# Split-weight buffers 32 bytes longer: their starting places run through the multiples of 32 within 128

## The chip, the cores and the metric

The kernel runs on one core of a Trainium2 chip. The metric is the device time of one execution in microseconds (us), the median of three runs. One further execution was taken with the hardware profiler; all rows below are from that one.

## What is computed

The reference is a two-layer decoder trunk in float32 on 256 tokens of width 2048. Each layer normalises its input, multiplies it by `w_in`, runs eight heads of latent attention and eight heads of retention, joins them through `w_o`, and adds a squared-ReLU MLP of width 8192:

```python
for l in range(DEPTH):
    h = rmsnorm(x, attn_norm[l])
    proj = h @ w_in[l]
    c_q, c_kv, k_rope, rq, rk, rv, rg = jnp.split(proj, split_pts, axis=-1)
    a = mla_attention(c_q, c_kv, k_rope, q_norm[l], kv_norm[l], w_uq[l], w_ukv[l], cos64, sin64)
    r = retention(rq, rk, rv, rg, cos128, sin128)
    mixed = jnp.concatenate([rmsnorm(a, beta_attn[l]), r * beta_ret[l]], axis=-1)
    x = x + mixed @ w_o[l]
    h = rmsnorm(x, mlp_norm[l])
    x = x + jnp.square(jax.nn.relu(h @ w_up[l])) @ w_down[l]
return rmsnorm(x, final_norm)
```

## The kernel before

Activations lie transposed in SBUF, features on the partitions, 256 tokens along the row. To keep float32 accuracy with a fast matmul format (float32r), every operand is split into a head and a remainder. A weight block of 512 KB is loaded into one of five `raw` buffers, ScalarE writes its head (L195) and VectorE its remainder (L196) into one of six rotating buffers `w`, each 2048 elements long plus 2 * MOVING = 32 elements of room; one more buffer, `wh`, has 1024 plus 32. TensorE then runs three kinds of matmul on them, and it does this in the order in which the code is written, with the weights of the next matmul loaded (PEld) while the present one runs:

- L229 and L230 (`mac_feat`), always as a pair: the weights in `w` are the stationary operand of 128 columns, and the activations move: 512 columns (head and remainder of the activations, head of the weights), then 256 columns (remainder of the weights). The moving tiles are `xs` (normalised input, also under the name `ms` in the code), `u` (MLP activations), `mix`, `cq` and `ckv`.
- L234 and L235 (`mac_tok`), also a pair of 512 and 256 columns, but the other way round: `w` moves, and `xs` or `ckv` is stationary. L383 to L385 do likewise with 320 columns.
- L730 (`seven_products`): `w` or `wh` moves in runs of 512 columns, and `u` or the sums `f` of it are stationary. 21 such matmuls make a step. Only here the weights lie MOVING = 16 elements (64 bytes) behind the start of their buffer.

L850 is a run of matmuls near the end that read `u` as both operands and whose result nobody uses.

Tiles are placed one behind the other, in the order of their pools, at multiples of 32 bytes. The places that matter are therefore given as the start within 128 bytes (the address modulo 128, as the built program has it). Before the change:

| tile | place before | place after |
|---|---|---|
| `x`, `xs`, `tab`, `ssq` | 96 | 96 |
| `raw` | 64 | 64 |
| `w`, the six buffers | 64, 64, 64, 64, 64, 64 | 64, 96, 0, 32, 64, 96 |
| `wh` | 64 | 0 |
| `w` and `wh` as L730 reads them | 64 bytes further than the two rows above | 64 bytes further |
| `sq`, `t`, `tb` (temporaries) | 64 | 32 |
| `u`, `f`, `mix`, `cq`, `ckv`, `p` and other tiles of a layer | 96 | 64 |

Within a `w` buffer every slice that a matmul reads starts at a multiple of 512 bytes, so all of them have the place of their buffer.

Of the kernel before, what the change touches and what calls it, by code (L numbers as in the profile page):

```python
# [12 lines left out]
F32R = mybir.dt.float32r  # L13
# [5 lines left out]
P = 128  # L19
# [27 lines left out]
MOVING = 16  # L47
# [46 lines left out]
def kernel(ctx: ExitStack, tc: tile.TileContext, xt, positions, w_in, w_uq, w_ukv, w_o, w_up, w_down,  # L94
# [5 lines left out]
    wpool = ctx.enter_context(tc.tile_pool(name="w", bufs=1))  # L100
# [10 lines left out]
    def tmp(tag="t", bufs=6):  # L111
        return tpool.tile([P, T], F32, tag=tag, name=tag, bufs=bufs)


    def w_tile(shape, moving=False):
        n = math.prod(shape[1:])
        o = MOVING if moving else 0
        tag, size, bufs = ("wh", 1024, 1) if moving and n <= 1024 else ("w", max(n, 2048), N_SPLIT)
        t = wpool.tile([P, size + 2 * MOVING], F32R, tag=tag, name=tag, bufs=bufs)[:, o:o + n]
        names = "abc"[:len(shape) - 1]  # L120
        return t.rearrange(f"p ({' '.join(names)}) -> p {' '.join(names)}", **dict(zip(names, shape[1:])))

# [93 lines left out]
    def stream(w, r0, c0, nk, width=256, kc=None, backward=False):  # L216

        kc = kc or 1024 // width
        for s in reversed(range(0, nk, kc)) if backward else range(0, nk, kc):
            raw = early.pop(0) if early else w_load(w[r0 + s * P:r0 + (s + kc) * P, c0:c0 + width], [P, kc, width])  # L220
            ws = w_tile([P, kc, 2, width])
            split_w(ws[:, :, 0, :], ws[:, :, 1, :], raw)
            for k in range(kc):
                yield s + k, ws[:, k]
            weave()
# [125 lines left out]
    for l in range(DEPTH):  # L351
        g0 = l * G_LAYER

        with tc.tile_pool(name=f"mix{l}", bufs=1) as ap:
# [13 lines left out]
            for c0 in range(COL_CQ, COL_CKV, 256):  # L368
                for ps in proj_feat(w_in[l], 0, c0, xs, backward=l > 0):
                    t = tmp()  # L370
# [74 lines left out]

            def mla(i):
                wr = w_tile([P, 4, 2, P])
                wn = []
                for kk in range(0, 4, 2):
                    raw = w_load(w_uq[l][kk * P:(kk + 2) * P, i * 384:(i + 1) * 384], [P, 2, 384])  # L450
                    wu = raw.rearrange("p k (h c) -> p k h c", h=2)
                    ws = w_tile([P, 2, 2, 256])
                    wv = ws.rearrange("p k s (h c) -> p k s h c", h=2)
                    for k in range(2):
                        wrv = wr[:, kk + k].rearrange("p s (a h c) -> p s a h c", a=2, h=2)
                        src = wu[:, k, :, 128:192].rearrange("p h (a c) -> p a h c", a=2)
                        split_w(wrv[:, 0], wrv[:, 1], src)
                    split_w(wv[:, :, 0], wv[:, :, 1], wu[:, :, :, 0:128])
                    wn += [ws[:, 0], ws[:, 1]]
# [187 lines left out]
            for c0, nt in OUT_GROUPS:  # L647
                for n, ps in enumerate(proj_feat(w_o[l], 0, c0 * P, mixed, nt)):
                    j = c0 + n
                    t = tmp()  # L650
# [241 lines left out]
```

## Time and profile before

| | |
|---|---|
| median of three runs | 2172.16 us (2171.9 to 2172.17) |
| profiled execution | 2172.12 us |
| its span, first to last instruction | 2170.3 us |
| TensorE busy | 2135.7 us, 98% |
| VectorE busy | 1789.4 us, 82% |
| ScalarE busy | 1300.3 us, 60% |
| mean granted TensorE clock | 0.994 of full speed |

About 2 us lie outside the span. A matmul's listed duration includes the time in which its results drain, during which the next matmul already runs. How fast TensorE goes is therefore read from the distance between the starts of matmuls, and the listed durations say only how forms compare.

### The profile page before, as it was taken

The numbers are of one execution on the slowest core, as the hardware profiler recorded it, in microseconds if no ns is written. First come the engines' busy times: TensorE is split into PE (matmuls) and PEld (weight loads), VectorE is DVE, ScalarE is ACT, GpSimd is POOL, SyncE is SP. The second block draws the span as 40 slices with busy tenths as digits, with TensorE's granted clock in tenths as the row PEclk, the third lists the DMA queues.
The fourth block names the chain that finished last, engine by engine and source line by source line (L and its number), as shares of the span: only waits on it lengthen the run. The fifth ranks groups of instructions, "written<-read, shape, count | busy, mean of one in ns | idle before, by whom it ended". The sixth has DMA issues, their size and how long they took to land.

```text
span 2170.3 us, 32892 instructions
## 1 busy us (share of the span) xinstructions
PE 2135.7 (98%) x11926; PEld 1861.6 (86%) x11926; DVE 1789.4 (82%) x3183; ACT 1300.3 (60%) x2234; POOL 107.0 (5%) x130
## 2 busy tenths in 40 slices
PE   7999999999999999999899999999999999999997
PEld 6888888888888888888688888888888888888886
DVE  8878976788689779879968888676986887898797
ACT  7455545565676566566645555456665655665665
POOL 4000000001001001100000000000010010010000
PEclk9999999999999999999999999999999999999998
DMA  7555456658757857855465555566587577577663
GB/s 247 171 161 174 147 189 196 184 168 227 235 165 216 241 165 217 247 176 173 148 200 159 165 173 165 183 189 186 169 236 219 167 224 236 165 217 224 181 194 107
DMA packets 364771, 412.69 MB, mean 190 GB/s; under 512 B 14144, under 2 KB 284608, under 8 KB 364608
## 3 DMA queue, kind: packets, MB, share of 16 engines
q1 hardware_dynamic: 349824, 397.08, 59.7%
q0 software_dynamic: 13824, 12.59, 3.9%
q8 instruction: 93, 1.52, 0.3%
q10 hardware_dynamic: 960, 0.92, 0.1%
q14 instruction: 70, 0.57, 0.1%
HBM read 395.85 MB, written 2.10 MB: 183 GB/s over the span
## 4 chain that ended last, share of the span: by engine, by line
PE 88%; DVE 7%; ACT 2%; issue 1%; DMA 1%; SPq 0%; DVEq 0%; ACTq 0%
PE mm L229 43%; PE mm L230 22%; PE mm L730 11%; PE mm L234 3%; DVE w L196 2%; DVE raw L716 2%; PE mm L235 1%; PE at L229 1%; ACT w L195 1%; DMA raw<-w_down 1%; PE at L230 1%; PE at L500 0%; PE at L499 0%; PE mm L383 0%; PE mm L384 0%
## 5 line engine op out<-in xcount | busy, mean ns | idle before, releaser
L195 ACT CAST w<-raw 128x1024 fp32r<-128x1024 f32 (+2 forms) x856 | 847.1, 1007 | 656.8 <-PE mm L230 363.2
L196 DVE TENSOR_TENSOR w<-raw,w 128x1024 fp32r<-128x1024 f32 (+2 forms) x856 | 987.1, 1170 | 291.9 <-ACT w L195 286.1
L229 PE MATMUL mm<-xs,w 128*128 128x512 f32 x2944 | 1034.2, 394 | 8.5 <-ACT w L195 8.3
L230 PE MATMUL mm<-xs,w 128*128 128x256 f32 x2944 | 827.4, 281 | 4.4 <-DVE w L196 4.4
L229 PEld LDWEIGHTS mm<-xs,w 128*128 128x128 f32 x2944 | 553.8, 188 | 127.8 <-ACT w L195 8.6
L230 PEld LDWEIGHTS mm<-xs,w 128*128 128x128 f32 x2944 | 556.0, 189 | 7.5 <-DVE w L196 7.1
L229 PE MATMUL mm<-u,w 128*128 128x512 f32 x1024 | 360.7, 393 | 0.2 <-ACT w L195 0.2
L230 PE MATMUL mm<-u,w 128*128 128x256 f32 x1024 | 288.8, 282 | 6.4 <-DVE w L196 6.4
L229 PEld LDWEIGHTS mm<-u,w 128*128 128x128 f32 x1024 | 193.2, 189 | 43.0 <-ACT w L195 0.7
L230 PEld LDWEIGHTS mm<-u,w 128*128 128x128 f32 x1024 | 194.0, 189 | 10.0 <-DVE w L196 7.3
L730 PE MATMUL mm<-w,f 128*128 128x512 f32 x768 | 191.1, 396 | 2.2 <-ACT w L195 1.2
L716 DVE TENSOR_TENSOR raw<-raw 128x512 f32<-128x512 f32 x256 | 176.8, 691 | 6.6
L229 PE MATMUL mm<-mix,w 128*128 128x512 f32 x512 | 178.0, 391 | 0.0
L730 PEld LDWEIGHTS mm<-w,f 128*128 128x128 f32 x768 | 144.0, 188 | 38.9 <-ACT w L195 2.1
L820 POOL DMA_DIRECT2D x<-t x96 | 83.4, 869 | 1863.0 <-ACT t L819 1561.9
L230 PE MATMUL mm<-mix,w 128*128 128x256 f32 x512 | 143.7, 281 | 0.0
L247 ACT COPY tb<-mm 128x256 f32<-128x256 f32 x232 | 82.5, 371 | 63.0 <-PE mm L230 59.3
L229 PEld LDWEIGHTS mm<-mix,w 128*128 128x128 f32 x512 | 96.1, 188 | 20.8
L730 PE MATMUL mm<-w,u 128*128 128x512 f32 x384 | 110.6, 396 | 0.0
L248 DVE TENSOR_TENSOR t<-mm,tb 128x256 f32<-128x256 f32 x232 | 91.4, 418 | 19.9 <-ACT tb L247 19.4
L230 PEld LDWEIGHTS mm<-mix,w 128*128 128x128 f32 x512 | 96.4, 188 | 0.0
L234 PE MATMUL mm<-w,xs 128*128 128x512 f32 x256 | 92.8, 401 | 0.0
(202 smaller groups left out, 1955.3 us busy)
## 6 DMA issues: line engine op xcount, KB each, us to landing
raw<-w_up SPq DMA_DIRECT2D x256, 512.0 KB, 4.4
raw<-w_down SPq DMA_DIRECT2D x256, 512.0 KB, 5.2
raw<-w_in SPq DMA_DIRECT2D x144, 512.0 KB, 4.5
raw<-w_o SPq DMA_DIRECT2D x64, 512.0 KB, 4.1
x<-t POOLq DMA_DIRECT2D x96, 128.0 KB, 5.7
raw<-w_uq SPq DMA_DIRECT2D x16, 384.0 KB, 4.3
raw<-w_in SPq DMA_DIRECT2D x16, 320.0 KB, 3.2
raw<-w_ukv SPq DMA_DIRECT2D x8, 512.0 KB, 4.3
```

The costliest lines, as they stand in the source:

```text
L195: nc.scalar.copy(dst_h, src)
L196: nc.vector.tensor_tensor(dst_l, src, dst_h.bitcast(F32), op=ALU.subtract)
L229: nc.tensor.matmul(ps, wk[:, 0, n0:n0 + P], act.rearrange("p s t -> p (s t)"), start=first, stop=False)
L230: nc.tensor.matmul(ps[:, 0:T], wk[:, 1, n0:n0 + P], act[:, 0, :], start=False, stop=last)
L234: nc.tensor.matmul(ps, act[:, 0, t0:t0 + P], wk, start=first, stop=False)
L235: nc.tensor.matmul(ps[:, 0:256], act[:, 1, t0:t0 + P], wk[:, 0], start=False, stop=last)
L247: nc.scalar.copy(tb, ps[:, T:2 * T])
L248: nc.vector.tensor_tensor(dst, ps[:, 0:T], tb, op=ALU.add)
L716: nc.vector.tensor_tensor(dst, dst, other, op=ALU.add)
L730: nc.tensor.matmul(ps[i], a[:, p, :], w[:, q, :], start=first and n == 0, stop=last and n == 2)
L820: nc.gpsimd.dma_start(x[j], t, accum_op=ALU.add)
```

## The change

`w_tile` makes each buffer 8 elements (32 bytes) longer. A `w` buffer was 2080 elements or 8320 bytes, which is 65 times 128, so all six had one place within 128. It is 8352 bytes now, and each buffer starts 32 bytes further within 128 than the one ahead of it. Everything that is placed behind the buffers moves by 7 * 32 = 224 bytes, that is 96 within 128; what stands ahead of them stays. The table above has the places that come of it. Nothing else is changed: on every engine the same instructions stand in the same order, with the same sizes, waits and transfers.

```diff
@@ -116,7 +116,7 @@
         n = math.prod(shape[1:])
         o = MOVING if moving else 0
         tag, size, bufs = ("wh", 1024, 1) if moving and n <= 1024 else ("w", max(n, 2048), N_SPLIT)
-        t = wpool.tile([P, size + 2 * MOVING], F32R, tag=tag, name=tag, bufs=bufs)[:, o:o + n]
+        t = wpool.tile([P, size + 2 * MOVING + 8], F32R, tag=tag, name=tag, bufs=bufs)[:, o:o + n]
         names = "abc"[:len(shape) - 1]
         return t.rearrange(f"p ({' '.join(names)}) -> p {' '.join(names)}", **dict(zip(names, shape[1:])))
```

## Rows read from the trace of the kernel before

**Rows 1.** The page's head: span, busy time of each engine, granted TensorE clock.

```profile
span 2170.3 us, 32892 instructions
...
PE 2135.7 (98%) x11926; PEld 1861.6 (86%) x11926; DVE 1789.4 (82%) x3183; ACT 1300.3 (60%) x2234; POOL 107.0 (5%) x130
...
PEclk9999999999999999999999999999999999999998
```

**Rows 2.** The page's chain that ended last, shares of the span.

```profile
PE 88%; DVE 7%; ACT 2%; issue 1%; DMA 1%; SPq 0%; DVEq 0%; ACTq 0%
```

**Rows 3.** The waits of TensorE, longest first: us in total, times, longest.

```profile
PE mm L230 <- DVE w L196: 10.8, 6, 6.4
PE mm L229 <- ACT w L195: 8.5, 3, 7.3
```

**Rows 4.** Groups by form, TensorE: count | busy us, mean ns | idle before.

```profile
L229 PE MATMUL mm<-xs,w 128*128 128x512 f32 x2944 | 1034.2, 394 | 8.5 <-ACT w L195 8.3
...
L229 PE MATMUL mm<-u,w 128*128 128x512 f32 x1024 | 360.7, 393 | 0.2 <-ACT w L195 0.2
...
L730 PE MATMUL mm<-w,f 128*128 128x512 f32 x768 | 191.1, 396 | 2.2 <-ACT w L195 1.2 <-DVE w L196 1.0
L229 PE MATMUL mm<-mix,w 128*128 128x512 f32 x512 | 178.0, 391 | 0.0
...
L730 PE MATMUL mm<-w,u 128*128 128x512 f32 x384 | 110.6, 396 | 0.0
L234 PE MATMUL mm<-w,xs 128*128 128x512 f32 x256 | 92.8, 401 | 0.0
...
L730 PE MATMUL mm<-wh,u 128*128 128x512 f32 x192 | 55.2, 396 | 0.0
L229 PE MATMUL at<-cq,w 128*128 128x512 f32 x96 | 34.6, 393 | 0.0
...
L234 PE MATMUL at<-w,ckv 128*128 128x512 f32 x32 | 11.6, 394 | 0.0
L229 PE MATMUL at<-ckv,w 128*128 128x512 f32 x32 | 11.5, 393 | 0.0
```

**Rows 5.** Timeline, TensorE, sixteen pairs of L229, L230: start us, us.

```profile
700.99 0.39 PE L229 MATMUL mm<-u,w 128*128 128x512 f32 x1
701.22 0.28 PE L230 MATMUL mm<-u,w 128*128 128x256 f32 x1
...
706.55 0.86 PE L730 MATMUL mm<-wh,u 128*128 128x512 f32 x3
```

**Rows 6.** Timeline, TensorE, two runs of eight pairs of L234, L235.

```profile
212.73 0.39 PE L234 MATMUL mm<-w,xs 128*128 128x512 f32 x1
...
215.53 0.39 PE L234 MATMUL at<-w,ckv 128*128 128x512 f32 x1
...
216.93 0.39 PE L234 MATMUL mm<-w,xs 128*128 128x512 f32 x1
...
219.75 0.39 PE L499 MATMUL at<-kn,qn 128*128 128x128 f32 x2
```

**Rows 7.** Chain in order of time, steps of L730: start us, us, count.

```profile
858.26 4.92 PE mm L730 x21
...
879.21 4.88 PE mm L730 x21
```

**Rows 8.** Timeline, TensorE, the run of L850 near the end.

```profile
2149.30 3.15 PE L850 MATMUL mm<-u,u 128*128 128x512 f32 x13
2152.29 0.28 PE L230 MATMUL mm<-u,w 128*128 128x256 f32 x1
```

**Rows 9.** Groups by form, VectorE.

```profile
L189 DVE TENSOR_TENSOR u<-t,u 128x256 fp32r<-128x256 f32 x128 | 50.4, 420 | 0.0
L196 DVE TENSOR_TENSOR wh<-raw,wh 128x512 fp32r<-128x512 f32 x64 | 43.8, 685 | 0.0
...
L196 DVE TENSOR_TENSOR w<-raw,w 128x512 fp32r<-128x512 f32 x16 | 11.0, 685 | 0.8 <-ACT w L195 0.8
```

## The prediction, made before the result was known

> **What bounds the kernel now.** I read the head of the page first: TensorE is busy 98% of the span, VectorE 82%, ScalarE 60%, and the granted clock is at its upper level, 2.4 GHz, in nearly every slice [rows 1]. Then the chain that ended last: 88% of it is TensorE [rows 2]. Then what TensorE waits for: the two longest entries, both for a split of weights, are 19.3 us together in nine stops [rows 3], under 1% of the span. So the time is the sum of the distances between the starts of matmuls, and nothing else can shrink or grow much without passing through them.
>
> How large is such a distance, against the columns alone? A pair of L229 and L230 streams 512 + 256 = 768 columns, 320 ns at 2.4 GHz. Sixteen pairs start from 700.99 to 706.55 us [rows 5], 5.56 / 16 = 347.5 ns a pair. So 27.5 ns of a pair are not columns. A step of L730 has 21 matmuls in 4.88 to 4.92 us [rows 7], 232.4 to 234.3 ns each, 233.3 in the middle, against 213.3 ns for 512 columns: 20.0 ns over. L850 ran 13 matmuls of 512 columns from 2149.30 to 2152.29 us [rows 8], 230.0 ns each.
>
> So matmuls of one size do not have one distance, and what differs between the lines is which tile moves, which one is stationary, and the places of both. I sort them by one number, the place of the moving tile less the place of the stationary one, modulo 128 (the table of places gives it): 96 - 64 = 32 for all pairs of L229 and L230; 0 - 96, which is also 32, for L730; 0 for L850; 64 - 96, that is 96, for L234 and L235. Two runs of eight pairs of L234 take 2.80 and 2.82 us [rows 6], 350.0 and 352.5 ns, although their columns are those of L229's pairs. That is 2.5 and 5.0 ns more, 3.75 in the middle. L850 against L730 is 3.3 ns less. Neither comparison is clean: in L234 the tiles also have exchanged their roles, and L850 runs where little else does. But the sizes bound what a place can be worth here: some ns of a pair of 347.
>
> **The change, part by part.** No instruction, transfer or wait is added, removed or moved, so there are only places to price.
>
> *VectorE, ScalarE, transfers.* The split of 512 elements takes 685 ns with its output at place 64 (`w`) and 685 ns at place 0 (`wh`), and 420 ns for 256 elements with tiles at 64 and 96 [rows 9]. I see no dependence on the place and cost this at nothing. Place 32 for the temporaries is in no row here; should it cost some per cent of these operations, the cover is VectorE's idle 18% and ScalarE's 40% of the span [rows 1]. `raw` and `x`, into which weights and inputs are loaded, keep their places.
>
> *The pairs of L229 and L230.* With `xs` moving there are 2944 of them; with `u`, `mix`, `cq` and `ckv` 1024 + 512 + 96 + 32 = 1664 [rows 4]. The six buffers are taken in turn, so a sixth of the pairs falls to each. With `xs` at 96 the distances of places become 32, 0, 96, 64, 32, 0: a third of the pairs (981) stays at 32, 1472 come to 0 or 64, 491 come to 96. With `u` and the others at 64 they become 0, 96, 64, 32, 0, 96: 832 at 0 or 64, 555 at 96, 277 still at 32.
>
> A pair that comes to 96 costs 3.75 ns more by the rows of L234: (491 + 555) * 3.75 ns = 3.9 us. For pairs at 0 or 64 no row exists. Below: the 512-column part alone was 3.3 ns cheaper at 0 than at 32 in the other pattern (L850 against L730), so a gain of 3.3 ns is not excluded. Above: 5.0 ns, the worse run of L234. Between these I take a loss of 2.5 ns, nearer to the upper end, because L234 alternates 512 and 256 columns as these pairs do, and L850 does not; its row is the farther one. That is (1472 + 832) * 2.5 ns = 5.8 us, with ends of -7.6 and +11.5 us.
>
> *L730.* `u` and `f` go to 64. Of its 768 + 384 = 1152 matmuls on `w` [rows 4], the moving slice is at 0, 32, 64, 96, 0, 32, so the distance becomes 64, 96, 0, 32, 64, 96. The 192 on `wh` come to 0. At 0 I take L850's distance, 3.3 ns less: (192 + 192) * 3.3 = -1.3 us. At 64 and 96 (768 matmuls) the bounds are -3.3 and +5.0 ns, that is -2.5 and +3.8 us, from the same rows; I take nothing, since they have both signs and neither row is nearer.
>
> *L234 and L235.* 256 + 32 = 288 pairs [rows 4] leave the distance 96 in two thirds of the cases. 43 with `xs` and 11 with `ckv` come to 32 and regain 3.75 ns each, the rest some 1 ns: -0.4 us.
>
> **The sum:** 3.9 + 5.8 - 1.3 - 0.4 = +8.0 us. The profiled execution took 2172.12 us, so 2180.1 us; it stands 0.04 us under the median of the three runs, so I forecast 2180 us for the median, 0.4% slower. A slower TensorE gives the splits more time, so some of the 19.3 us of waits may shrink; I count none of it, since they are nine long stops and not many short ones.
>
> **The rivals.**
>
> *The places do not matter (2172 us).* The 2.5 to 5.0 ns of L234 could belong to the exchange of roles and not to the places, and L850's to its quiet surroundings. Then every pair stays at 347.5 ns, every matmul of L730 at 233.3, and the time is 2172. For it speaks that no line here shows two places of the same tile side by side. Against it: the rows differ by up to 5 ns at equal columns and at the same clock, and an exchange of roles would need a reason of its own. The same result comes if losses and gains cancel, or if the unknown distances cost nothing: then 3.9 - 1.3 - 0.4 = +2.2 us, 2174. The Trainium skill, page "TensorE: Matmul & The Clock Gate", section "Step-by-step: what each phase is for", has a rule that speaks for this rival: TensorE has two independent read ports, so "Loading the next tile's weights doesn't steal SBUF read bandwidth from the running matmul". By that rule a stationary tile's place could not change the distance and the sum would be zero; this trace does not decide it, but 27.5 ns over the columns in each pair sit badly with it.
>
> *The unknown distances are the better ones (2166 us, faster).* If 0 and 64 gain in the pairs what L850 shows against L730, the 2304 pairs gain 7.6 us and the 768 matmuls of L730 at 0 or 64 gain 2.5 us; the pairs at 96 still lose 3.9 us. The sum is -6.2 us, 2166 us. It decides from the point where a pair at 0 or 64 gains 2.5 ns: 2304 * 2.5 ns = 5.8 us, with L730's 2.5 us, less 3.9 us, are 4.4 us, 0.2%. For it speaks the one row at distance 0; against it, that it is another pattern of columns.
>
> *Pairs at 0 or 64 are much worse (2199 us).* The mean listed duration of L234 is 401 ns against 391 for L229 with `mix` [rows 4], 10 ns; a part of that is waiting. If 0 or 64 cost 10 ns a pair, 2304 pairs lose 23 us, and with the 3.9 us of the others the time is 2199. For it speaks that the moving and the stationary stream would then meet at the same place from the first column on; against it, again L850, which does so at 230.0 ns.
>
> **How the numbers follow.** Forecast of a small loss, 2176.5 to 2187: 0.46. No effect, or effects that cancel: 0.28. Faster: 0.16. Much slower: 0.10. Two executions of one kernel differ by far less than 0.2% (4.3 us), but a difference under that is about what a measurement of this kernel cannot tell from no change. So faster has 0.16, same 0.28, slower 0.46 + 0.10 = 0.56. The range from 2165 to 2194 us reaches over the faster case, and on the other side to the worst of the forecast (11.5 us for 0 and 64, 5.2 for 96 at 5.0 ns, 3.8 in L730, about 20 us) and a little more; it leaves out the much slower case, and the tail of the faster one.
>
> **What would show it.** In the profile after, runs of L229 and L230 should have two or three distances, by the buffer that holds the weights: 347.5 ns for buffers whose place is 32 under the moving tile's, and around 350 to 352 for the others, changing with each block of weights. L234's runs should come down to 347.5 ns for one buffer in six. L730's steps should spread wider than 4.88 to 4.92 us. VectorE's and ScalarE's mean durations should stay within 1%. The forecast is wrong if all pairs keep one distance, if they fall under 347.5 ns, or if VectorE's or ScalarE's operations grow and TensorE's waits with them.

## The result

The changed kernel takes 2183.47 us, median of four runs (2183.31 to 2183.87), against 2172.16 us: the ratio is 1.0051, with a 95% interval of 1.0038 to 1.0063. That is slower by about 11.3 us, on the side that was forecast and inside the range; the forecast was 8 us.

The page of the kernel after, its head: span, busy time of each engine, and the chain that ended last.

```profile
span 2181.6 us, 32892 instructions
...
PE 2146.9 (98%) x11926; PEld 1862.7 (85%) x11926; DVE 1790.4 (82%) x3183; ACT 1302.7 (60%) x2234; POOL 108.0 (5%) x130
...
PEclk9999999999999999999999999999999999999998
...
PE 90%; DVE 6%; ACT 2%; issue 1%; DMA 1%; SPq 0%; DVEq 0%; ACTq 0%
```

The span has grown by 2181.6 - 2170.3 = 11.3 us [rows 1], and TensorE's busy time by 11.2 us. VectorE's grew by 1.0 us and ScalarE's by 2.4 us. TensorE's growth alone is that of the span, so the difference lies there, at the same granted clock (0.994 before, 0.995 after). Its waits for splits have hardly changed, 12.4 + 7.4 = 19.8 us now against 19.3 before [rows 3]:

```profile
PE mm L230 <- DVE w L196: 12.4, 5, 6.4
PE mm L229 <- ACT w L195: 7.4, 2, 7.1
```

The groups by form of VectorE and ScalarE after:

```profile
L196 DVE TENSOR_TENSOR w<-raw,w 128x1024 fp32r<-128x1024 f32 x792 | 955.6, 1223 | 294.3 <-ACT w L195 288.4 <-PE mm L730 1.3
...
L189 DVE TENSOR_TENSOR u<-t,u 128x256 fp32r<-128x256 f32 x128 | 50.3, 419 | 0.1
L196 DVE TENSOR_TENSOR wh<-raw,wh 128x512 fp32r<-128x512 f32 x64 | 43.8, 684 | 0.0
...
L195 ACT CAST w<-raw 128x1024 fp32r<-128x1024 f32 x792 | 818.4, 1049 | 640.8 <-PE mm L230 341.2 <-DVE raw L716 172.4 <-DMA raw<-w_down 40.0
```

The two large groups of splits before, which [rows 9] does not have:

```profile
L196 DVE TENSOR_TENSOR w<-raw,w 128x1024 fp32r<-128x1024 f32 x792 | 955.4, 1223 | 285.3 <-ACT w L195 279.8 <-PE mm L730 1.4
...
L195 ACT CAST w<-raw 128x1024 fp32r<-128x1024 f32 x792 | 818.6, 1049 | 634.9 <-PE mm L230 344.1 <-DVE raw L716 165.6 <-DMA raw<-w_down 40.5
```

These means are those of before to within 1 ns, although `t`, the source of `u`, now stands at place 32 and the outputs in `w` at four places. So the splits, which are most of these engines' work, do not mind the place.

TensorE does. Here is the timeline after, two stretches of sixteen pairs of L229 and L230; each stretch uses two buffers, eight pairs each, and the first pair of each buffer is shown.

```profile
705.32 0.39 PE L229 MATMUL mm<-u,w 128*128 128x512 f32 x1
...
708.10 0.40 PE L229 MATMUL mm<-u,w 128*128 128x512 f32 x1
...
710.92 0.88 PE L730 MATMUL mm<-wh,u 128*128 128x512 f32 x3
...
715.83 0.40 PE L229 MATMUL mm<-u,w 128*128 128x512 f32 x1
...
718.63 0.39 PE L229 MATMUL mm<-u,w 128*128 128x512 f32 x1
...
721.41 0.85 PE L730 MATMUL mm<-wh,u 128*128 128x512 f32 x3
```

In the order of the buffers: 2.78 us for the buffer whose distance is 32, 2.82 at distance 0, 2.80 at distance 96, 2.78 at 32 again. By eight pairs these are 347.5, 352.5, 350.0 and 347.5 ns. One kernel, one engine, only `u` tiles moving, and the pace changes with the buffer that holds the weights.

For all pairs I take the starts of the instructions in the two traces and sort the time from one pair to the next by the distance of the places, here modulo 256, which splits each distance in two. Stops, more than 25 ns above the median of a group, are left out of the means. The same for single matmuls of L730. Means in ns, with the counts of all intervals:

```
pairs of L229, L230     before              after, xs moving    after, others moving
distance 32, 160        347.0 to 347.3      347.1 to 347.3      347.4
distance 0                                  350.8  x479         352.6  x276
distance 128                                350.0  x477         349.7  x223
distance 192 (64)                           351.6  x511         352.3  x303
distance 96, 224                            350.8  x456         350.6  x599
L730                    233.6 (32, 160)     232.4 (all of them, 231.7 to 233.3)
L234, L235              350.6 (96, 224)     351.3 (all of them)
```

The excess over 347.1 ns, times the counts, is 9.1 us for the distances 0 and 64 (0, 128 and 192 in the table), and 3.7 us for 96. L730 gives back 1344 * 1.2 ns = 1.6 us, and L234 loses 288 * 0.7 ns = 0.2 us. The sum is 11.4 us, and the spans differ by 11.3. L234 after, sorted in the same way, follows the distance too: 347.0 and 347.5 ns at 32 and 160, but 352.6 and 350.9 at 0 and 128, 353.0 at 64, 350.4 and 352.2 at 96 and 224.

### The profile page after: what moved, and what is told of

Same layout as the page of the kernel before. It is cut to its first block, busy times and chain, and to the rows that moved or that the text cites. A ratio compares the mean times of both kernels' runs of the same rounds, so it can differ in the third digit from the quotient of the medians.

```text
span 2181.6 us, 32892 instructions
## 1 busy us (share of the span) xinstructions
PE 2146.9 (98%) x11926; PEld 1862.7 (85%) x11926; DVE 1790.4 (82%) x3183; ACT 1302.7 (60%) x2234; POOL 108.0 (5%) x130
## 4 chain that ended last, share of the span: by engine, by line
PE 90%; DVE 6%; ACT 2%; issue 1%; DMA 1%; SPq 0%; DVEq 0%; ACTq 0%
PE mm L229 44%; PE mm L230 23%; PE mm L730 11%; PE mm L234 3%; DVE w L196 2%; DVE raw L716 2%; PE mm L235 1%; PE at L229 1%; ACT w L195 1%; DMA raw<-w_down 1%; PE at L230 1%; PE at L500 0%; PE at L499 0%; PE mm L383 0%; PE mm L385 0%
## 5 line engine op out<-in xcount | busy, mean ns | idle before, releaser
L229 PE MATMUL mm<-xs,w 128*128 128x512 f32 x2944 | 1041.8, 396 | 7.3 <-ACT w L195 7.1
L230 PE MATMUL mm<-xs,w 128*128 128x256 f32 x2944 | 827.4, 281 | 6.0 <-DVE w L196 6.0
L229 PEld LDWEIGHTS mm<-xs,w 128*128 128x128 f32 x2944 | 554.2, 188 | 133.2 <-ACT w L195 7.4
L230 PEld LDWEIGHTS mm<-xs,w 128*128 128x128 f32 x2944 | 555.7, 189 | 8.8 <-DVE w L196 8.4
L229 PE MATMUL mm<-u,w 128*128 128x512 f32 x1024 | 364.2, 396 | 0.2 <-ACT w L195 0.2
L230 PE MATMUL mm<-u,w 128*128 128x256 f32 x1024 | 289.0, 282 | 6.4 <-DVE w L196 6.4
L229 PEld LDWEIGHTS mm<-u,w 128*128 128x128 f32 x1024 | 193.3, 189 | 46.1 <-ACT w L195 0.7
L230 PEld LDWEIGHTS mm<-u,w 128*128 128x128 f32 x1024 | 193.8, 189 | 10.0 <-DVE w L196 7.3
L730 PE MATMUL mm<-w,f 128*128 128x512 f32 x768 | 190.1, 395 | 1.9 <-ACT w L195 1.0
L229 PE MATMUL mm<-mix,w 128*128 128x512 f32 x512 | 179.7, 395 | 0.0
L730 PEld LDWEIGHTS mm<-w,f 128*128 128x128 f32 x768 | 143.9, 188 | 37.6 <-ACT w L195 1.9
L230 PE MATMUL mm<-mix,w 128*128 128x256 f32 x512 | 143.8, 281 | 0.0
L229 PEld LDWEIGHTS mm<-mix,w 128*128 128x128 f32 x512 | 96.1, 188 | 22.4
L730 PE MATMUL mm<-w,u 128*128 128x512 f32 x384 | 110.2, 394 | 0.0
L230 PEld LDWEIGHTS mm<-mix,w 128*128 128x128 f32 x512 | 96.4, 188 | 0.0
L234 PE MATMUL mm<-w,xs 128*128 128x512 f32 x256 | 92.9, 401 | 0.0
```

Source lines behind the costliest of these rows:

```text
L229: nc.tensor.matmul(ps, wk[:, 0, n0:n0 + P], act.rearrange("p s t -> p (s t)"), start=first, stop=False)
L230: nc.tensor.matmul(ps[:, 0:T], wk[:, 1, n0:n0 + P], act[:, 0, :], start=False, stop=last)
L234: nc.tensor.matmul(ps, act[:, 0, t0:t0 + P], wk, start=first, stop=False)
L730: nc.tensor.matmul(ps[i], a[:, p, :], w[:, q, :], start=first and n == 0, stop=last and n == 2)
```

## The experiments

The theory is that the distance of the two places modulo 128 sets the pace. Its rivals: the place of one tile by itself; the temporaries or layer tiles that moved along; the step from one place to another between buffers; the length itself. Each edit below is against the kernel before; ratios are to it, on the same chip.

**Only the buffers.** `wh` gets 64 bytes so that all tiles behind keep their places.

```diff
-        t = wpool.tile([P, size + 2 * MOVING], F32R, tag=tag, name=tag, bufs=bufs)[:, o:o + n]
+        t = wpool.tile([P, size + 2 * MOVING + (16 if tag == "wh" else 8)], F32R, tag=tag, name=tag, bufs=bufs)[:, o:o + n]
```

> Only the six w buffers (and wh) change their places; everything behind them is brought back to its old place. Theory (what costs is the distance of the moving tile's place from the stationary tile's, modulo 128): all 4608 pairs of L229 and L230 now have the distances 32, 0, 96, 64, 32, 0 by buffer, so two thirds of them leave 32 and lose the 3.5 to 4.8 ns that the changed kernel shows; about +11 us, 2183, as much as the whole change. Rival (the loss comes from the temporaries at place 32, or from u, mix and f at 64): those are back, and the time is near 2172, or keeps only the share of the pairs with xs if both take part (about 2179).

Measured: 2180.75 us, 1.0041 (1.0027 to 1.0055). The buffers' places alone bring 8.2 us, where about 11 were expected. Sorted by distance as above, the pairs did lose 11.1 us; L730, which the expectation left out, gave back 1.7 (232.3 ns in the mean against 233.6). The tiles behind stand where they were, so most of the loss does not need them.

**Only what lies behind.**

```diff
-        t = wpool.tile([P, size + 2 * MOVING], F32R, tag=tag, name=tag, bufs=bufs)[:, o:o + n]
+        t = wpool.tile([P, size + 2 * MOVING + (24 if tag == "wh" else 0)], F32R, tag=tag, name=tag, bufs=bufs)[:, o:o + n]
```

> Only what lies behind the buffers moves by 96 bytes; the w buffers all stay at 64. Theory of the distance: the 1664 pairs with u, mix, cq and ckv all come to distance 0 and lose about 4 ns each, +6.6 us; L730 comes to distance 64 and gains about 1.8 ns on 1344 matmuls, -2.4 us; the sum is +4 us, 2176; the pairs with xs stay at 347 ns. Rival (it is the step from one place to another between buffers that costs): no buffer differs from another, so 2172.

Measured: 2177.04 us, 1.0019 (1.0009 to 1.0028). No buffer differs from another here, and it still costs about 4.5 us, near the 4 that were expected: the pairs with `u`, `mix`, `cq` and `ckv` went to 350.8 and 351.3 ns (distances 128 and 0), those with `xs` stayed at 347.0 to 347.3. So the step between buffers is not needed for a loss.

**Everything shifted by 32 bytes.**

```diff
-LONGER_ONES, LONGER_XS, LONGER_ROOT = 8, 24, 23
+LONGER_ONES, LONGER_XS, LONGER_ROOT = 16, 24, 23
```

> Everything from the tables on moves by 32 bytes together, so all distances are as before and every place is another: moving tiles at 0, w at 96. Theory of the distance: 2172, and 347 ns a pair. Rival (the place of one operand by itself, such as 96 for the weights, costs): a pair loses some 4 ns and the time is near 2190.

Measured: 2173.01 us, 1.0003 (0.9993 to 1.0012). The weights stand at 96 and the moving tiles at 0, and no change shows. These places by themselves cost nothing.

**One distance for all pairs: 0, 64, 96.** `raw` and `w` are moved by the length of the last `xs` tile, and `wh` is lengthened so that the tiles behind stay where they were.

```diff
-LONGER_ONES, LONGER_XS, LONGER_ROOT = 8, 24, 23
+LONGER_ONES, LONGER_XS, LONGER_ROOT = 8, 32, 23
...
-        t = wpool.tile([P, size + 2 * MOVING], F32R, tag=tag, name=tag, bufs=bufs)[:, o:o + n]
+        t = wpool.tile([P, size + 2 * MOVING + (24 if tag == "wh" else 0)], F32R, tag=tag, name=tag, bufs=bufs)[:, o:o + n]
```

That is distance 0. For 64 the two numbers are 48 and 8, for 96 they are 40 and 16.

> All w buffers (with raw) at 96 and the moving tiles at 96: every pair of L229 and L230 at distance 0, L730 at 64, L234 at 0. Theory of the distance: 4608 pairs lose about 3.8 ns, +17.5 us, L730 gains about 2.4 us; 2187. Rival (the step between buffers costs): 2172. Rival (a place of 96 for the weights costs): as much as in the run in which all places are shifted.

> All w buffers (with raw) at 32, moving tiles at 96: every pair of L229 and L230 at distance 64, L730 at 0, L234 at 64. By the distances of the changed kernel 4608 pairs lose 4.8 ns, +22 us, L730 gains 1.3 ns on 1344 matmuls, -1.8 us: 2192. Rival (at 128 and at 0 the collision is worst and 64 lies as far from it as can be): no loss, 2172 or less.

> All w buffers (with raw) at 0, moving tiles at 96: every pair of L229 and L230 at distance 96, L730 at 96, L234 at 32. By the distances of the changed kernel 4608 pairs lose 3.5 ns, +16 us, L730 nothing, the 288 pairs of L234 gain 3.3 ns, -1 us: 2187. Rival (distance 96 was dear in L234 only because the weights moved there): no loss, 2171.

Measured: 2187.12 us at 0, 1.0069 (1.0054 to 1.0084); 2195.21 us at 64, 1.0102 (1.0088 to 1.0116); 2189.55 us at 96, 1.0075 (1.0061 to 1.0089). Expected were 2187, 2192 and 2187 us. All three are slower, by 14.6, 22.5 and 16.8 us, and 64 is the dearest, as among the buffers of the changed kernel. At distance 0 the weights stand at 96, as in the run before this one, which cost nothing: so it is the distance that costs, and not the place of the weights. `raw` moves along in these three runs; in the runs at 16 and 48 below it stays, and they lose as much. The first pair of each of the two buffers of one stretch, in the timeline with all pairs at 64:

```profile
707.97 0.39 PE L229 MATMUL mm<-u,w 128*128 128x512 f32 x1
...
710.77 0.40 PE L229 MATMUL mm<-u,w 128*128 128x512 f32 x1
...
713.61 0.85 PE L730 MATMUL mm<-wh,u 128*128 128x512 f32 x3
```

That is 350.0 and 355.0 ns a pair in this stretch, whose two buffers stand at distances 192 and 64 within 256; all pairs together ran at 352.7 ns in the mean (351.8 to 353.3 by group), 5.6 over the 347.1 of before. The run with the pairs at 96 has L234 at distance 32. Its timeline, two runs of eight pairs as in [rows 6]:

```profile
213.77 0.39 PE L234 MATMUL mm<-w,xs 128*128 128x512 f32 x1
...
216.54 0.39 PE L234 MATMUL at<-w,ckv 128*128 128x512 f32 x1
...
217.93 0.39 PE L234 MATMUL mm<-w,xs 128*128 128x512 f32 x1
...
220.71 0.38 PE L499 MATMUL at<-kn,qn 128*128 128x128 f32 x2
```

2.77 and 2.78 us, 346.3 and 347.5 ns a pair, where it was 350.0 and 352.5; the means over all of its pairs are 347.3 and 347.4 ns. So what made L234 slower than L229 before was the distance, and not that weights move there.

**128 bytes longer instead of 32.**

```diff
-        t = wpool.tile([P, size + 2 * MOVING], F32R, tag=tag, name=tag, bufs=bufs)[:, o:o + n]
+        t = wpool.tile([P, size + 2 * MOVING + 32], F32R, tag=tag, name=tag, bufs=bufs)[:, o:o + n]
```

> The buffers are 128 bytes longer instead of 32, so every place modulo 128 is as before. Theory of the distance: 2172, the same. Rival (the length itself, or where the buffers lie at large, costs): about 2175 or more.

Measured: 2171.54 us, 0.9994 (0.9985 to 1.0003). The interval takes in 1: a loss from the length itself, or from the place at large, does not show.

**Half steps: 16 and 48.**

```diff
-        o = MOVING if moving else 0
+        o = MOVING if moving else 4
```

That is distance 16; with 28 in place of 4 it is 48.

> The weights that stay in the pairs of L229 and L230 start 16 bytes into their buffer, so their place is 80 and every pair has distance 16, between 0 (about +3.8 ns) and 32 (0); L730 is as before, L234 comes to 112. If only the 32-byte piece in which a tile starts counts, a pair costs what it costs at 0 or what it costs at 32: 2187 or 2172. If the distance counts byte by byte, something between: about 2180.

> The same with 112 bytes: place 48, every pair at distance 48, between 32 (0) and 64 (+4.8 ns). Pieces of 32 bytes: 2172 or 2195. Byte by byte: about 2183.

Measured: 2187.38 us at 16, 1.0068 (1.0055 to 1.0082), and 2190.45 us at 48, 1.0083 (1.0069 to 1.0096). At 16 the time is that of distance 0, as pieces of 32 bytes would have it, but the pairs show that this is a coincidence: at 16 within 256 they ran at 347.7 to 348.8 ns, close to those at 32, and at 144 at 352.6 to 352.9. At 48 the time is neither that of 32 nor that of 64 nor halfway (349.6 to 349.7 ns at 48 within 256, 352.6 to 352.9 at 176). So neither reading of the distance holds. Over both halves of 256 together 32 is a narrow best among the places that were run, and 16 bytes to either side cost 15 to 18 us.

**The two other lines, put at better distances.** L730's slices start 96 bytes into the buffer (distance 64), the weights of the retention values 64 bytes (distance 32).

```diff
-    def w_tile(shape, moving=False):
+    def w_tile(shape, moving=0):
...
-        o = MOVING if moving else 0
+        o = moving
...
-    def stream(w, r0, c0, nk, width=256, kc=None, backward=False):
+    def stream(w, r0, c0, nk, width=256, kc=None, backward=False, moving=0):
...
-            ws = w_tile([P, kc, 2, width])
+            ws = w_tile([P, kc, 2, width], moving)
...
-                for k, wk in stream(w_in[l], 0, COL_RV + 256 * i, KD):
+                for k, wk in stream(w_in[l], 0, COL_RV + 256 * i, KD, moving=MOVING):
...
-                    ws = w_tile([P, 2, n], True)
+                    ws = w_tile([P, 2, n], 24)
```

> The kernel before, with two distances set by what the changed kernel showed: the slices that move in L730 start 96 bytes into their buffer, so that their distance is 64 and no longer 32 (1.8 ns less on 1344 matmuls, -2.4 us), and the weights that L234 moves for the retention values start 64 bytes into theirs, distance 32 and no longer 96 (3.3 ns less on 256 pairs, -0.8 us). Theory: 2169, 0.15% faster. Rival (what L730 showed at 64 in the changed kernel came from other buffers changing around it): 2172.

Measured: 2169.41 us, 0.9984 (0.9975 to 0.9993), as expected: a gain of 3 us, with an interval below 1. L730 ran at 230.1 ns at distance 64 within 256 and 233.0 at 192, so the two halves of 256 are not alike for it.

**All distances chosen, within 256.** The last edit, against which the lines here stand, with buffers 128 bytes longer (so that all six have one place within 256) and L730's slices 160 bytes into them.

```diff
-        t = wpool.tile([P, size + 2 * MOVING], F32R, tag=tag, name=tag, bufs=bufs)[:, o:o + n]
+        t = wpool.tile([P, size + 2 * MOVING + 32], F32R, tag=tag, name=tag, bufs=bufs)[:, o:o + n]
...
-                    ws = w_tile([P, 2, n], 24)
+                    ws = w_tile([P, 2, n], 40)
```

> Buffers 128 bytes longer, so that all six have one place within 256 as well; the pairs stay at 32 (160 within 256). L730's slices start 160 bytes into their buffer, which puts all its 1344 matmuls at distance 0 within 256, where the run with all pairs at 64 showed 230.0 ns against 233.3 to 233.9; the retention values move at distance 32. Theory: the run with 128 bytes more took 2171.5; 1344 * 3.4 ns = 4.6 us less in L730 and 0.8 us less in L234 give 2166, 0.25% faster than the kernel before. Rival (256 does not matter, only 128): L730 at 0 shows the mean of what it showed at 0 and 128, about 231 ns, and the time is 2167.5.

Measured: 2165.74 us, 0.9968 (0.9956 to 0.9980): this kernel beats both, and the rival's 2167.5 us lies above all six of its times (2164.45 to 2165.99). Its chain in order of time, the first steps of L730:

```profile
470.48 4.79 PE mm L730 x21
480.82 4.79 PE mm L730 x21
491.16 4.79 PE mm L730 x21
```

4.79 / 21 = 228.1 ns, and every one of the 52 steps listed has 4.79 us, where before they ran from 4.88 to 4.92 [rows 7]. The gain of L730 is 1344 * (233.6 - 228.1) ns = 7.4 us, more than the 4.6 expected; its stops grew from 3.7 to 5.9 us at the same time, so that the total agrees with the forecast in part by luck.

## Why the prediction was right

*What bounds the kernel.* Shown: the span grew by 11.3 us and TensorE's busy time by 11.2, VectorE's by 1.0 and ScalarE's by 2.4. The waits of 19.3 us took up none of the loss; they are 19.8 us after.

*No cost on VectorE and ScalarE.* Right: 1223, 419 and 684 ns on VectorE and 1049 ns on ScalarE after, within 1 ns of before, place 32 included.

*The pairs at distance 96:* 3.9 us forecast, 3.7 measured. The row that it came from, L234, was the right one, and the doubt whether its roles or its places made it slow is settled by the run that moved L234 to distance 32.

*The pairs at 0 and 64:* 5.8 us forecast, 9.1 measured. This is the term that was mis-sized: 2.5 ns a pair was taken between two bounds, and 4.0 was paid, nearer still to L234's 5.0; with all pairs at 64 it was 5.6, beyond that bound. The lower bound, L850's gain at distance 0, was from another pattern, as the text said, and does not carry over: at distance 0 runs of 512 columns gain (L730: 230.0 and 228.1 ns in two runs) while pairs of 512 and 256 columns lose.

*L730:* -1.3 us forecast, -1.6 measured, and that they agree is luck. The 384 matmuls at distance 0 (0 and 128 within 256) were to gain 3.3 ns each; they ran at 232.3 and 231.7 ns against 233.6, which is 0.6 us and not 1.3. Those at 64 were costed at nothing and gained 0.7 us (231.7 and 232.1 ns); the rest gained 0.3. The steps spread wider, as the prediction said, and most came down:

```profile
485.04 4.85 PE mm L730 x21
...
516.51 4.91 PE mm L730 x21
```

*L234:* -0.4 us forecast, +0.2 measured. Its pairs at 32 came down to 347.5 ns as forecast, but those at 0 and 64 did not gain 1 ns: they rose to 350.9 to 353.0. It is too small to matter.

*The rival of no effect* fell with the run at distance 0: the same instructions, 14.6 us more, while shifting everything together changed nothing. The rule that was quoted for it, from the Trainium skill, page "TensorE: Matmul & The Clock Gate", section "Step-by-step: what each phase is for", is that loading the next tile's weights takes no read bandwidth from the running matmul; if it means that the two places are independent, it does not hold for this kernel. The measurement decides: a stationary tile's place against the moving tile's is worth up to 1.0% of the time here. *The faster rival* was right in sign for L730 and wrong for the pairs, which are more of the time. *The rival of 10 ns a pair* did not occur: the dearest uniform distance, 64, cost 5.6 ns a pair, of which L730 gave back some 3.5 us (230.0 and 232.2 ns), so that 22.5 us were left.

What stays open is what collides. That the moving reads of a matmul and the loading of the next weights meet in the same part of the memory would fit, since only their difference matters, but it is not shown: no run here separates the weights being loaded from those in use, and the narrowness of the best place (48 is dear, and 16 in one half of 256) and its dependence on the pattern of columns are not explained.

## What to carry to other kernels

Where TensorE is busy 98% and its pairs stand further apart than their columns, compare the starts of equal matmuls from different lines: a few ns between them can be a difference of places, which costs nothing to change. A buffer's length is part of a kernel's tuning: lengthen it, and everything behind it moves; keep the difference of moving and stationary places in mind, per line (the best one differs by the pattern of columns, so it has to be measured), and set it with an offset into the buffer, as the last kernel here does (0.3% under the kernel before).

## What the runs showed that was not expected

The best distance differs by the pattern of columns. With 512 and 256 columns in turn 32 is best (346.7 to 347.4 ns for L229's pairs in all kernels, 349.6 to 353.3 at 0, 48, 64 and 96). Nearly all of the loss falls into the matmul of 512 columns: from the start of L229 to that of L230 it is 229.3 ns before, and in the changed kernel 229.4 at 32, 232.5 at 0, 233.7 at 64 and 232.8 at 96, while the 256 columns of L230 take 117.8 to 118.2 ns everywhere in these two. With 512 columns alone 0 is the best that was run (228.1 ns with all buffers at 0 within 256, against 233.0 to 234.0 at 32 in the kernels whose buffers share one place). So 512 columns come near 229 ns at the best place of either pattern and take 233 to 234 at a bad one; it is the place that differs. With 320 columns the place made little difference: the matmuls of L383 to L385 start 146.6 to 146.8 ns apart before, where all distances are 96, and 146.4 to 147.3 after, where they take four values. (Their slices start at multiples of 1280 bytes, not of 512, which leaves them the place of their buffer all the same.) And 128 bytes are not the whole period: where all buffers share one place within 128, L730 at distance 64 ran at 229.6 to 230.1 ns, and at 192 at 233.0 to 233.4. In the changed kernel, where the buffers differ, the same two are 231.7 and 232.1.
